# Sums over eight selections as trees of three contiguous additions

## The chip, the cores and the metric

One core of a Trainium2 chip. The metric is the device time of one execution in microseconds (us), the median of three runs.

## The reference

One encoder layer on 1024 tokens of width 1024, in float32: a combined projection, two groups of attention heads (windowed, and on a 2-D neighbourhood), an output projection and a layer norm; then PEER, a layer of 16384 single-neuron experts with product keys, and a second layer norm. PEER is where the edit lies. For each token and each of 8 heads two sets of 128 scores are cut to their top 16; the 256 sums of pairs are cut to their top 16 again, and each of these 16 names one expert:

```
cand_idx = i_top[:, :, 0, :, None] * PEER_N_KEYS + i_top[:, :, 1, None, :]
fs, fpos = lax.top_k(cand, PEER_TOPK)
eidx = jnp.take_along_axis(cand_idx, fpos, axis=-1)
g = jax.nn.softmax(fs, axis=-1)
```

The output of PEER is the sum over a token's 128 experts of gelu(x . u) * g * v.

## The kernel before

The tokens are eight tiles of 128, one token a partition. The first part of the kernel projects, attends (two tiles at a time) and normalizes. After each pair of tiles `route` (L519) computes the scores of PEER for the pair, takes the top 16 of each set with `top16` (L122) and calls `decode` (L176) for each of the two tiles. Route of pair 0 comes before the attention of tiles 2 and 3, and so on; route of pair 3 is the last of this part.

The experts are computed in two ways. Tiles 0 to 4 (`ND` = 5) go through all experts densely: a matrix of gates, nearly all of it zero, is multiplied in between two matmuls (`hstage` L707, `vmm` L733). For tiles 0 and 1 (`NS` = 2) this matrix is written in DRAM (`gs`) by `scatter` (L160): 256 indirect DMAs issued by GpSimd, each adding 128 single gates at the computed places, 16 for each tile and head, the heads of both tiles in turn (L576 to L578). For tiles 2 to 4 `build` (L582) makes it with one-hot matmuls and stores it in `gd` (L617). Tiles 5 to 7 gather their experts' rows one by one with indirect DMAs (L656) during the dense part, and VectorE multiplies and adds them.

The dense part starts with `load_g` (L696): on SyncE's queue a load of gates from `gs`, which waits for the scatters of every head, and one from `gd`. The raw blocks of the experts' weights (L709, L727) follow on the same queue. ScalarE casts a block (L86), VectorE subtracts (L87), and TensorE multiplies (L91 to L93, L736 to L738).

In `decode` everything but one exponential is VectorE's. It makes a table of the candidates (L183, L185), takes their top 16 and positions (L190), and turns a position into the index of an expert by selections. Sixteen steps compare all positions with the starts of the rows and multiply with a difference of indices (L203; the first is L201), sixteen others pick the index of the second key (L217). Each writes one of the eight slices of `big` (128 partitions x 8 slices x 8 heads x 16); after every eight a reduction sums over the slices (L206, L221) into `ef` or `e2`. The slices lie 512 bytes apart, and the reduction reads them with the slice as the innermost dimension:

```
bsum = big.rearrange("p a h k -> p h k a")
...
if a % 8 == 7:
    nc.vector.tensor_reduce(ef if a == 7 else e2, bsum, AX.X, OP.add)
```

`big`, `ef` and `e2` have one buffer each, which every call of `decode` uses. A call has four reductions, and there are eight calls. L207 and L222 add the two halves; L210 to L215 split the sum in row and remainder; L224 (tiles 2 to 7) or L226 and L227 (tiles 0 and 1) write the indices.

The order of the instructions on each engine isn't that of the text: it is laid out when the program is built, by a planner with durations of its own for every instruction (L859, `schedule_with_timeline_sim=True`). VectorE's instructions of `decode` stand in it between those of attention, `top16`, `build` and the start of the dense part. On the chip each engine then keeps to its order.

Of the kernel before, what the change touches and what calls it, by code (L numbers as in the profile page):

```python
# [17 lines left out]
OP = mybir.AluOpType  # L18
AX = mybir.AxisListType
# [38 lines left out]
def trunk(ctx, tc, x, xt, wqk, wo, gn, sink, biasa, biasb, ln, wq, keyst, uv, ut, vt, out):  # L58
    nc = tc.nc
# [62 lines left out]
    def top16(vals, idx, src, pool, n):  # L122
        tmp = pool.tile([P, P], F32, name="t16")
        nc.vector.max(vals[:, 0:8], src)
        nc.vector.max_index(idx[:, 0:8], vals[:, 0:8], src)
        nc.vector.match_replace(tmp[:, :n], vals[:, 0:8], src, BIG)
        nc.vector.max(vals[:, 8:16], tmp[:, :n])
        nc.vector.max_index(idx[:, 8:16], vals[:, 8:16], tmp[:, :n])
# [47 lines left out]
    def decode(idx, g, sv, iv, pool, t=None):  # L176
        s2 = sv.rearrange("p (h two) k -> p h two k", two=2)
        fi = pool.tile([P, 8, 2, TOPK], F32, name="fi", bufs=1)
        nc.vector.tensor_copy(fi, iv.rearrange("p (h two) k -> p h two k", two=2))
        cv = pool.tile([P, 8, NCAND], F32, name="cv", bufs=1)  # L180
        for a in range(8):
            w = WIDTHS[a]
            nc.vector.tensor_tensor(cv[:, :, OFFS[a]:OFFS[a] + w], s2[:, :, 1, 0:w],  # L183
                                    s2[:, :, 0, a:a + 1].to_broadcast([P, 8, w]), OP.add)
        nc.vector.tensor_tensor(cv[:, :, NCAND - 8:], s2[:, :, 0, 8:16],  # L185
                                s2[:, :, 1, 0:1].to_broadcast([P, 8, 8]), OP.add)
        fs = pool.tile([P, 8, TOPK], F32, name="fs", bufs=1)
        pos = pool.tile([P, 8, TOPK], U32, name="pos", bufs=1)
        for h in range(8):
            top16(fs[:, h, :], pos[:, h, :], cv[:, h, :], pool, NCAND)  # L190
        pf = pool.tile([P, 8, TOPK], F32, name="pf", bufs=1)
        nc.vector.tensor_copy(pf, pos)
        dlt = pool.tile([P, 8, TOPK - 1], F32, name="dlt", bufs=1)
        nc.vector.tensor_sub(dlt, fi[:, :, 0, 1:], fi[:, :, 0, 0:TOPK - 1])
        nc.vector.scalar_tensor_tensor(dlt, dlt, 64.0, wrow[:, None, :].to_broadcast([P, 8, TOPK - 1]),
                                       op0=OP.mult, op1=OP.add)
        big = pool.tile([P, 8, 8, TOPK], F32, name="big", bufs=1)
        ef = pool.tile([P, 8, TOPK], F32, name="ef", bufs=1)
        e2 = pool.tile([P, 8, TOPK], F32, name="e2", bufs=1)
        bsum = big.rearrange("p a h k -> p h k a")  # L200
        nc.vector.tensor_scalar(big[:, 0, :, :], fi[:, :, 0, 0:1].to_broadcast([P, 8, TOPK]), 64.0, None, op0=OP.mult)  # L201
        for a in range(1, TOPK):
            nc.vector.scalar_tensor_tensor(big[:, a % 8, :, :], pf, START[a] - 0.5,  # L203
                                           dlt[:, :, a - 1:a].to_broadcast([P, 8, TOPK]), op0=OP.is_ge, op1=OP.mult)
            if a % 8 == 7:
                nc.vector.tensor_reduce(ef if a == 7 else e2, bsum, AX.X, OP.add)  # L206
        nc.vector.tensor_add(ef, ef, e2)  # L207
        ei = pool.tile([P, 2, 8 * TOPK], I32, name="ei", bufs=1)
        e0 = ef.rearrange("p h k -> p (h k)")
        nc.vector.tensor_copy(ei[:, 0, :], e0)  # L210
        nc.vector.tensor_scalar(ei[:, 1, :], ei[:, 0, :], 63, None, op0=OP.bitwise_and)
        nc.vector.tensor_scalar(ei[:, 0, :], ei[:, 0, :], 6, 7, op0=OP.logical_shift_right, op1=OP.logical_shift_left)
        of = pool.tile([P, 2, 8, TOPK], F32, name="of", bufs=1)
        nc.vector.tensor_copy(of.rearrange("p a h k -> p a (h k)"), ei)
        nc.vector.tensor_sub(pf, pf, of[:, 1])  # L215
        for b in range(TOPK):
            nc.vector.scalar_tensor_tensor(big[:, b % 8, :, :], pf, float(b),  # L217
                                           fi[:, :, 1, b:b + 1].to_broadcast([P, 8, TOPK]),
                                           op0=OP.is_equal, op1=OP.mult)
            if b % 8 == 7:  # L220
                nc.vector.tensor_reduce(ef if b == 7 else e2, bsum, AX.X, OP.add)  # L221
        nc.vector.tensor_add(ef, ef, e2)  # L222
        if t is None:
            nc.vector.tensor_add(idx.rearrange("p (h k) -> p h k", h=8), ef, of[:, 0])  # L224
        else:
            nc.vector.tensor_scalar(ef, ef, float(P * GC), base[:, t:t + 1], op0=OP.mult, op1=OP.add)  # L226
            nc.vector.scalar_tensor_tensor(idx.rearrange("p (h k) -> p h k", h=8), of[:, 0], GC / P, ef,  # L227
                                           op0=OP.mult, op1=OP.add)
        gv = g.rearrange("p (h k) -> p h k", h=8)
        nc.vector.tensor_tensor(gv, fs, fs[:, :, 0:1].to_broadcast([P, 8, TOPK]), OP.subtract)  # L230
        nc.scalar.activation(g, g, AF.Exp)
        gs = pool.tile([P, 8], F32, name="gs")
        nc.vector.tensor_reduce(gs, gv, AX.X, OP.add)
        nc.vector.reciprocal(gs, gs)
        nc.vector.tensor_mul(gv, gv, gs[:, :, None].to_broadcast([P, 8, TOPK]))
# [4 lines left out]
    with ExitStack() as att:  # L240
# [278 lines left out]
        def route(pr):  # L519
# [48 lines left out]
            for t in tiles:  # L568
                if t >= ND:
                    decode(eidx[t], gate[t], stop_[t], itop[t], rs)  # L570
                    continue
                idx = rs.tile([P, P], I32, name="idxd", bufs=4)
                g = rs.tile([P, P], F32, name="gated", bufs=4)
                decode(idx, g, stop_[t], itop[t], rs, t if t < NS else None)
                (dense if t < NS else todo).append((t, idx, g))
# [99 lines left out]
    total = NG * P // NB  # L675
# [31 lines left out]
    def hstage(e, pend):  # L707
        raw = dn.tile([P, KT, P], F32, name="raw", bufs=3)
        nc.sync.dma_start(raw, ut[e])  # L709
        uh = dn.tile([P, KT, P], F32R, name="uh")  # L710
        ul = dn.tile([P, KT, P], F32R, name="ul")
        split(uh, ul, raw)
        gl = dn.tile([P, DN], F32, name="gl")
        for j, (o, n) in enumerate(hch):
            ps = ph.tile([P, 512], F32, name="h")
            for k in range(KT):
                mm3(ps[:, :n], uh[:, k, :], ul[:, k, :], dh[:, k, o:o + n], dl[:, k, o:o + n], k == 0, k == KT - 1)
            nc.scalar.activation(gl[:, o:o + n], ps[:, :n], AF.Gelu)  # L718
            if j == (e == ne - 1) and pend is not None:
                vres(*pend)  # L720
        glv = gl.rearrange("p (q c) -> p q c", c=GC)
        nc.vector.tensor_mul(glv, glv, gt[e // EG][:, :, e % EG, :])
        ah = dn.tile([P, DN], F32R, name="ah", bufs=3)
        al = dn.tile([P, DN], F32R, name="al", bufs=3)
        split(ah, al, gl)
        raw = dn.tile([P, D], F32, name="raw", bufs=3)
        nc.sync.dma_start(raw, vt[e * P:(e + 1) * P, :])  # L727
        vh = dn.tile([P, D], F32R, name="vh", bufs=3)
        vl = dn.tile([P, D], F32R, name="vl", bufs=3)
        split(vh, vl, raw)  # L730
        return ah, al, vh, vl
# [39 lines left out]
    for e in range(ne):  # L771
        if e % EG == 0 and e + EG < ne:
            load_g(e // EG + 1)
        a = hstage(e, pend)
# [88 lines left out]
```

## Time and profile before

| | |
|---|---|
| median of three runs | 2978.63 us (2978.54 to 2978.84) |
| the profiled execution | 2985.32 us |
| its span, first to last instruction | 2981.6 us |
| mean granted clock of TensorE | 0.961 |
| TensorE busy | 2733.9 us (92%) |
| VectorE busy | 2408.1 us (81%) |
| ScalarE busy | 1202.3 us (40%) |
| GpSimd busy | 1065.1 us (36%) |

The profile is of one execution; its span is the time from the first to the last instruction of the program, and 3.7 us of its time lie outside it. Busy shares are means over the whole span, in which the parts of the kernel differ much, so the rows below are mostly of single stretches. In the rows PE is TensorE, DVE VectorE, ACT ScalarE, POOL GpSimd, SP SyncE; a q behind the name is the engine's sequencer, which issues DMAs and waits.

### The profile page before, as it was taken

How to read it: one execution, taken by the hardware profiler on the slowest of the kernel's cores; microseconds unless marked ns; L12 is line 12 of the kernel's file. 1: busy time of each engine (PE TensorE's matmuls, PEld its weight loads, DVE VectorE, ACT ScalarE, POOL GpSimd, SP SyncE). 2: the span in 40 equal slices, each digit the busy share in tenths (PEclk: the TensorE clock that was granted, in tenths of full speed). 3: DMA queues.
4: the chain of work that ended last, by engine and by line, in shares of the span. 5: the costliest groups of instructions: out<-in, count | busy, mean ns of one | idle time of the engine just before them, and what ended most of it. 6: DMA issues, size and time to landing. Idle time of an engine off the chain costs nothing.

```text
span 2981.6 us, 43327 instructions
## 1 busy us (share of the span) xinstructions
PE 2733.9 (92%) x15569; PEld 2357.3 (79%) x15569; DVE 2408.1 (81%) x5427; ACT 1202.3 (40%) x2486; POOL 1065.1 (36%) x732
## 2 busy tenths in 40 slices
PE   6887899897997867999999999999999999999996
PEld 4776577575785766888998899898888898988885
DVE  2344267887979988898998989999989999998965
ACT  2343154342786762333333343333333333333332
POOL 1111001078888881333333323333333333333300
PEclk8998989898997988999999999999999999999998
DMA  7688598897977767988998989998998898998851
GB/s 233 200 271 269 177 322 296 260 262 180 267 223 221 220 161 265 348 331 324 353 331 332 332 329 335 336 347 334 330 344 327 321 353 322 342 349 332 329 210 46
DMA packets 384886, 854.37 MB, mean 287 GB/s; under 512 B 83616, under 2 KB 243360, under 8 KB 333728
## 3 DMA queue, kind: packets, MB, share of 16 engines
q0 software_dynamic: 124224, 433.43, 41.3%
q1 hardware_dynamic: 230816, 388.82, 38.5%
q10 hardware_dynamic: 29632, 29.37, 3.1%
q8 instruction: 122, 2.00, 0.3%
q14 instruction: 92, 0.75, 0.1%
HBM read 765.21 MB, written 86.11 MB: 286 GB/s over the span
## 4 chain that ended last, share of the span: by engine, by line
PE 48%; DVE 5%; DMA 4%; issue 3%; ACT 2%; POOL 1%; SPq 0%; ACTq 0%; POOLq 0%; DVEq 0%
PE h L91 9%; PE h L92 8%; PE h L93 8%; PE po L736 5%; PE po L737 5%; PE po L738 5%; PE fl L737 3%; PE fl L736 3%; PE fl L738 3%; DMA uv<-in_uv_dram,eidx 2%; DMA raw<-in_ut_dram 2%; DVE uv L658 1%; DVE acc L668 1%; POOL uv L656 1%; DVE vl L87 1%
## 5 line engine op out<-in xcount | busy, mean ns | idle before, releaser
L656 POOL DMA_INDIRECT uv<-in_uv_dram,eidx x384 | 570.4, 1486 | 1162.5 <-DVE acc L668 688.5
L91 PE MATMUL h<-dh,uh 128*128 128x320 f32 x2048 | 641.3, 313 | 49.0 <-ACT uh L86 25.6
L93 PE MATMUL h<-dh,ul 128*128 128x320 f32 x2048 | 634.6, 310 | 0.8 <-DVE ul L87 0.8
L92 PE MATMUL h<-dl,uh 128*128 128x320 f32 x2048 | 634.1, 310 | 0.0
L658 DVE SCALAR_TENSOR_TENSOR uv<-uv,xg 128x1024 f32<-128x1024 f32 x384 | 467.4, 1218 | 43.1 <-DMA uv<-in_uv_dram,eidx 37.3
L165 POOL DMA_INDIRECT gs<-gated,idxd x256 | 434.9, 1699 | 171.3 <-DMA qlo<-wqd 87.0
L668 DVE SCALAR_TENSOR_TENSOR acc<-uv,hh,acc 128x1024 f32<-128x1024 f32 x381 | 487.6, 1280 | 4.3
L91 PEld LDWEIGHTS h<-dh,uh 128*128 128x128 f32 x2048 | 385.7, 188 | 83.7 <-ACT gl L718 48.6
L92 PEld LDWEIGHTS h<-dl,uh 128*128 128x128 f32 x2048 | 385.9, 188 | 10.9
L93 PEld LDWEIGHTS h<-dh,ul 128*128 128x128 f32 x2048 | 385.7, 188 | 4.9 <-DVE ul L87 1.5
L736 PE MATMUL po<-vh,ah 128*128 128x512 f32 x768 | 288.2, 391 | 1.5 <-ACT ah L86 1.5
L737 PE MATMUL po<-vl,ah 128*128 128x512 f32 x768 | 287.8, 391 | 0.0
L662 ACT ACTIVATE hh<-hh 128x1 f32<-128x1 f32 x384 | 77.6, 202 | 476.3 <-DVE uv L658 474.9
L738 PE MATMUL po<-vh,al 128*128 128x512 f32 x768 | 260.8, 391 | 0.0
L764 ACT COPY fl<-fl 128x512 f32<-128x512 f32 x252 | 147.1, 584 | 278.7 <-PE fl L738 278.5
L765 DVE TENSOR_TENSOR facc<-facc,fl 128x512 f32<-128x512 f32 x252 | 172.6, 685 | 72.8 <-ACT fl L764 72.6
L718 ACT ACTIVATE gl<-h 128x320 f32<-128x320 f32 x256 | 111.4, 435 | 254.5 <-PE h L93 244.4
L736 PE MATMUL fl<-vh,ah 128*128 128x512 f32 x512 | 201.8, 394 | 3.0 <-ACT fl L764 3.0
L737 PE MATMUL fl<-vl,ah 128*128 128x512 f32 x512 | 201.9, 394 | 0.0
L738 PE MATMUL fl<-vh,al 128*128 128x512 f32 x512 | 199.6, 390 | 0.0
L87 DVE TENSOR_TENSOR ul<-raw,uh 128x1024 fp32r<-128x1024 f32 x128 | 156.1, 1220 | 52.6 <-ACT uh L86 51.7
L86 ACT CAST uh<-raw 128x1024 fp32r<-128x1024 f32 x128 | 134.2, 1049 | 116.8 <-DMA raw<-in_ut_dram 60.7
(201 smaller groups left out, 5389.2 us busy)
## 6 DMA issues: line engine op xcount, KB each, us to landing
raw<-in_ut_dram SPq DMA_DIRECT2D x128, 512.0 KB
raw<-in_vt_dram SPq DMA_DIRECT2D x128, 512.0 KB
qhi<-wqd SPq DMA_DIRECT2D x48, 512.0 KB
qlo<-wqd SPq DMA_DIRECT2D x48, 512.0 KB
gd<-stage SPq DMA_DIRECT2D x12, 2048.0 KB
gt<-gd SPq DMA_DIRECT2D x32, 768.0 KB
wraw<-in_wqk_dram SPq DMA_DIRECT2D x36, 512.0 KB
bt<-in_biasb_dram SPq DMA_DIRECT2D x64, 288.0 KB
```

The lines of the kernel that those rows point to most:

```text
L87: nc.vector.tensor_sub(lo, raw, f(hi))
L91: nc.tensor.matmul(ps, wh, mh, start=first, stop=False)
L92: nc.tensor.matmul(ps, wh, ml, start=False, stop=False)
L93: nc.tensor.matmul(ps, wl, mh, start=False, stop=last)
L165: st = nc.gpsimd.indirect_dma_start(out=gs, out_offset=bass.IndirectOffsetOnAxis(ap=idx[:, k:k + 1], axis=0), in_=g[:, k:k + 1], in_offset ...
L656: nc.gpsimd.indirect_dma_start(out=u, out_offset=None, in_=uv, in_offset=bass.IndirectOffsetOnAxis(ap=eidx[t][:, k:k + 1], axis=0))
L658: nc.vector.scalar_tensor_tensor(u[:, 0:D], u[:, 0:D], 1.0, x1[t], op0=OP.mult, op1=OP.mult, accum_out=hh[:, k:k + 1])
L668: nc.vector.scalar_tensor_tensor(acc, u[:, D:], hh[:, k:k + 1], acc, op0=OP.mult, op1=OP.add)
L736: nc.tensor.matmul(ps, ah[:, cs], vh[:, js], start=first, stop=False)
L737: nc.tensor.matmul(ps, ah[:, cs], vl[:, js], start=False, stop=False)
L738: nc.tensor.matmul(ps, al[:, cs], vh[:, js], start=False, stop=last)
L765: nc.vector.tensor_add(acc[:, j, :], acc[:, j, :], fl)
```

## The change

Each of the two reductions at L206 and L221 becomes a call of a local function `total`, which adds the upper four slices of `big` onto the lower four, then the upper two of these onto the lower two, and then the two that are left into the destination. All three are additions on VectorE, over 512, 256 and 128 contiguous elements of each partition, and each reads what the one before it wrote. The view `bsum` goes. The sums are those of before, in another order.

```
-        bsum = big.rearrange("p a h k -> p h k a")
+
+        def total(dst):
+            nc.vector.tensor_add(big[:, 0:4], big[:, 0:4], big[:, 4:8])
+            nc.vector.tensor_add(big[:, 0:2], big[:, 0:2], big[:, 2:4])
+            nc.vector.tensor_add(dst, big[:, 0], big[:, 1])
+
...
             if a % 8 == 7:
-                nc.vector.tensor_reduce(ef if a == 7 else e2, bsum, AX.X, OP.add)
+                total(ef if a == 7 else e2)
...
             if b % 8 == 7:
-                nc.vector.tensor_reduce(ef if b == 7 else e2, bsum, AX.X, OP.add)
+                total(ef if b == 7 else e2)
```

## Rows read from the trace of the kernel before

**Rows 1.** Windows: us, then each engine's busy time (instructions), clock, DMA share, GB/s.

```profile
556.40:597.40 41.00, 35.82 (x254) 29.35 (x253) 41.00 (x199) 16.84 (x38) 0.00 (x0) 0.88 0.96 303
597.40:1107.70 510.30, 426.71 (x2893) 355.65 (x2891) 440.56 (x1861) 324.31 (x765) 427.11 (x252) 0.92 0.79 219
...
1133.30:1160.00 26.70, 22.84 (x119) 20.82 (x120) 24.94 (x52) 9.25 (x12) 0.90 (x1) 0.88 0.39 129
1200.00:2900.00 1700.00, 1680.02 (x9349) 1513.81 (x9348) 1540.91 (x2242) 612.34 (x1224) 554.17 (x372) 1.00 0.90 331
```

**Rows 2.** Chain that ended last, 1112 to 1132 us: start, us, what.

```profile
1112.73 1.55 POOL gs L165
...
1114.59 4.18 DMA gs<-gated,idxd
...
1119.07 0.37 SPq L700
...
1124.24 7.67 DMA raw<-in_ut_dram
```

**Rows 3.** Timeline of PE, after 1107 us: start, us, ..., [idle before <-releaser].

```profile
1133.34 0.64 PE L91 MATMUL h<-dh,uh 128*128 128x320 f32 x1 [25.65 <-ACT uh L86]
...
1159.62 0.41 PE L91 MATMUL h<-dh,uh 128*128 128x320 f32 x1 [1.57 <-ACT gl L718]
```

**Rows 4.** Timelines of DVE and POOL, 596 to 608 us.

```profile
596.37 0.28 DVE L227 SCALAR_TENSOR_TENSOR idxd<-of,ef 128x128 int32<-128x128 f32 x1
...
603.24 1.69 DVE L203 SCALAR_TENSOR_TENSOR big<-pf,dlt 128x128 f32<-128x128 f32 x8
...
605.38 1.91 DVE L206 TENSOR_REDUCE e<-big 128x128 f32<-128x1024 f32 x1
...
597.48 2.10 POOL L165 DMA_INDIRECT gs<-gated,idxd  x1 [87.00 <-DMA qlo<-wqd]
...
603.61 2.75 POOL L165 DMA_INDIRECT gs<-gated,idxd  x1 [0.31 <-issue]
606.66 1.55 POOL L165 DMA_INDIRECT gs<-gated,idxd  x1 [0.30 <-issue]
```

**Rows 5.** Line L165: xcount, duration ns min/median/max, first and last start.

```profile
L165 POOL DMA_INDIRECT gs<-gated,idxd x256: 1543/1547/5346, 597.5 to 1114.6; - x128
```

**Rows 6.** Groups from 597.4 to 1116.8 us: busy us, mean ns, idle before.

```profile
L165 POOL DMA_INDIRECT gs<-gated,idxd x256 | 434.9, 1699 | 171.3 <-DMA qlo<-wqd 87.0 <-issue 81.3 <-DMA gs<-gated,idxd 2.7
...
L203 DVE SCALAR_TENSOR_TENSOR big<-pf,dlt 128x128 f32<-128x128 f32 x87 | 18.4, 276 | 0.0
...
L206 DVE TENSOR_REDUCE e<-big 128x128 f32<-128x1024 f32 x6 | 11.4, 1897 | 0.0
```

**Rows 7.** Groups of DVE over the whole span.

```profile
L606 DVE TENSOR_TENSOR qj<-iota,tt 128x512 f32<-128x512 f32 x96 | 65.4, 681 | 0.0
...
L206 DVE TENSOR_REDUCE ef<-big 128x128 f32<-128x1024 f32 x8 | 15.2, 1904 | 0.0
...
L207 DVE TENSOR_TENSOR ef<-ef,e 128x128 f32<-128x128 f32 x8 | 2.2, 271 | 0.0
```

**Rows 8.** Timelines of DVE and ACT, 1151 to 1160 us (tile 7).

```profile
1151.84 1.98 DVE L221 TENSOR_REDUCE ef<-big 128x128 f32<-128x1024 f32 x1
1153.86 1.70 DVE L217 SCALAR_TENSOR_TENSOR big<-pf,fi 128x128 f32<-128x128 f32 x8
...
1157.95 0.29 DVE L224 TENSOR_TENSOR eidx<-ef,of 128x128 int32<-128x128 f32 x1
...
1159.13 0.44 ACT L718 ACTIVATE gl<-h 128x320 f32<-128x320 f32 x1 [8.90 <-DVE eidx L224]
```

**Rows 9.** Timeline of DVE, 572 to 575 us (tile 0).

```profile
572.29 0.21 DVE L210 CAST ei<-ef 128x128 int32<-128x128 f32 x1
...
573.77 0.20 DVE L211 TENSOR_SCALAR ei<-ei 128x128 int32<-128x128 int32 x1
...
574.26 0.20 DVE L212 TENSOR_SCALAR ei<-ei 128x128 int32<-128x128 int32 x1
```

## The prediction

> **What bounds the kernel now.** I read the trace by stages first. The decode of the expert choices, where the edit lies, runs between 556 and 1158 us of the span; from 1200 us on TensorE is busy for 1680.0 of 1700 us, so a gain or a loss here moves the end by as much as that last stage starts earlier or later, and nothing else counts [rows 1]. In 556 to 597 us VectorE has no idle time; from 597 to 1108 it is busy for 440.6 of 510.3 us and TensorE for 426.7, neither full, and GpSimd for 427.1 [rows 1]. None looks full, so the busy shares do not say which of them holds up the next stage.
>
> The chain of waits tells it: the last indirect scatter-add on GpSimd, its landing, the loads of the gates on SyncE, which wait for every scatter, and behind them on the same queue the first raw block, 7.67 us on its way [rows 2]. TensorE stands still for 25.65 us until that block has been cast [rows 3]. So VectorE, which is through with its work for TensorE by then, is not the bound; the scatters are. They form one almost unbroken line of 256, from 597.48 to the landing at 1118.77 us, and the first starts 0.8 us after VectorE has written the indices of tile 0 (L227 at 596.37) [rows 2, 4]. The time of the end is thus: end of tile 0's decode, plus the line of scatters, plus a fixed restart.
>
> What does a scatter cost? The median is 1.547 us [rows 5], with some 0.3 us before the next [rows 4], but the mean is 1.699 [rows 6]: 434.9 - 256 x 1.547 = 38.9 us are lost over the line. Put beside VectorE's timeline the loss shows its cause. The scatter at 603.61 us starts within a run of eight L203, each of which reads two operands in SBUF (pf and dlt); the run ends at 604.93 and the scatter takes 2.75, which is 1.2 us more than 1.55 and about what was left of the run. The scatter at 606.66 lies over a strided reduction, which reads one operand, and takes 1.55 [rows 4]. A scatter that starts while VectorE works with two operands from SBUF waits for it; over a reduction it does not.
>
> **The change part by part.** Each of 32 reductions (four a tile, eight tiles), 1.90 us [rows 7], becomes three additions over 512, 256 and 128 elements a partition. 512 cost 0.68 (L606) and 128 cost 0.27 (L207) [rows 7]; 256 are not shown, and between these two lies 0.41. Together 1.36 us. Operations that need not wait overlap: eight L203 of 0.276 take 1.69 us, so each start comes 0.07 before the end of the last [rows 4, 6]; directly dependent ones start 0.04 after it (L221 at 1151.84 ends at 1153.82, L217 starts at 1153.86) [rows 8]. So a tree takes 1.15 us of VectorE with other work between its steps and 1.44 without, against 1.83 to 1.94: a saving of 0.50 to 0.68 each, 16 to 22 us of VectorE's time. Nothing changes on the queues of SyncE, ScalarE and GpSimd: the edit issues no transfer. The waits it adds are those of each addition on the one before; behind them in order on VectorE stand attention and top-16 work of later tiles.
>
> (a) Four trees of tile 0 lie ahead of the first scatter, in the stretch where VectorE is full. Kept in place they bring it 4 x 0.68 = 2.7 us forward. But each tree has two more steps that wait for a step before. The order on VectorE is laid out ahead of time, and it puts work of other tiles between dependent steps: between L211 and L212 of tile 0 lie 0.49 - 0.13 = 0.36 us of it, between L210 and L211 1.48 - 0.14 = 1.34 [rows 9]. Eight new places at some 0.3 us, the shorter of these, give back 2.4. I take -0.3 us; the ends are -2.7 (no such work) and 8 x 0.85 - 2.7 = +4.1 us (the mean of the two).
>
> (b) 22 reductions lie in the stretch of the scatters: the group of six here and three more like it, of six, five and five [rows 6]. They held nothing up; 22 trees with two operands from SBUF will. Scatters start every 517.1 / 255 = 2.03 us (the first at 597.48, the last at 1114.59 [rows 2, 4]). One that starts at random within a hold of r us waits r/2 on average, and r / 2.03 of the starts fall in it, so a hold costs r x r / 4.06. Three holds of their own: (0.46 + 0.17 + 0.07) / 4.06 = 0.17 us a tree, 3.8 in all; one hold of 1.36: 0.46 a tree, 10.0 in all. Dependent additions leave a gap, so it should lie nearer the lower end: I take +5.0. The lower end is 0, if the starts happen to miss them.
>
> The Trainium skill bears on this. Its page SBUF — State Buffer, section Who interferes with whom, says that a VectorE instruction with two SBUF inputs contends with a GpSimd instruction that reads SBUF and that tensor_reduce on this chip never does; but it also infers that tensor_tensor leaves descriptor generation alone. By the first (b) is a loss, by the second nothing, and the sum would be -1.8 in place of +3.2 us; the two scatters above agree with the first.
>
> (c) The four trees of tile 7 lie after the restart. Its last index (L224 at 1157.95) releases a load on ScalarE, which held up the activation at 1159.13 for 8.90 us [rows 8], and TensorE waited 1.57 us for that [rows 3]. The four save some 2.0 us, of which TensorE can win back the 1.57: -1.5. The lower end is all of TensorE's idle time there, 26.7 - 22.84 = 3.9 us [rows 1], the upper +2.0, if work put into the new places undoes the saving and as much again.
>
> The 24 other trees free some 14 us of VectorE between 597 and 1130 us: worth nothing, since the scatters cover it; without that cover they would count. Nor do I count that the next batch could write four of the eight slices after the first addition.
>
> Sum: -0.3 + 5.0 - 1.5 = +3.2 us. Against the profiled execution, 2985.32 us (its span is 2981.6), that is 2988.5; the median of the runs shown is 2978.63, 6.7 below it, so I say 2981.8. About 0.2% (6.0 us) is what can be told from no change.
>
> **Rivals.** First, the scatters are not lengthened, and tile 0 comes early in full: -2.7 + 0 - 1.5 = -4.2, 2974.4 us, and up to 6.6 us faster with all idle time of (c). For it speaks that some runs of VectorE miss the starts; against it the 38.9 us lost already. The inference on the Trainium skill's page SBUF — State Buffer, section Who interferes with whom, comes to this rival. Second, on the slower side, the holds join: an addition beside a run of L203 or L602 and L606 makes one long hold, and the line of scatters grows by 10.0 or more. -0.3 + 10.0 - 1.5 = +8.2, 2986.8 us. It decides the case from (b) = 7.8 on, or 0.35 us a tree. For it speaks that a run of eight L203 was kept together and cost one scatter 1.2 us; against it the gap between dependent steps. Third, the layout puts more into the eight places of tile 0: +4.1 + 5.0 - 1.5 = +7.6, 2986.2 us. For it speaks that no two dependent steps of that decode shown stand side by side. Fourth, the change does not shorten VectorE's work: 1.44 against 1.90 would have to be wrong by a third; then (a) is the +2.4 of the new places, (c) is nothing, and with (b) it is +7.4, 2986.0 us.
>
> **How the numbers follow.** The forecast 0.48, the first rival 0.24, the second 0.13, the third 0.11, the fourth 0.04. Of the first some 0.17 lies beyond 6.0 us, an order laid out anew that also wins elsewhere among it; with the second, third and fourth in full and 0.03 from the upper part of the forecast, slower has 0.31; 0.52 is left for no change. The range goes from -6.6 (2972) to +13.4 (2992), short of all three upper ends at once.
>
> **What would show it.** Right: L206 and L221 gone, three groups of 32 at 0.68, 0.41 and 0.27 us; the first scatter between 595 and 598 us; the mean scatter up from 1.699 to about 1.72, its median still 1.547; the scatters longer than that lying over additions; TensorE's restart near 1138. Wrong: a mean scatter at 1.70 or below, a first scatter after 600 us, or a restart that no longer follows the landing of the last scatter.

## The result, and the profile after

The changed kernel takes 2998.47 us (median of 4 runs, 2991.39 to 3005.57); the kernel before, run beside it on the same chip, 2978.59. The ratio is 1.0075, with a 95% interval of 1.0055 to 1.0095: slower by some 20 us, beyond the upper end of the range. The profiled execution took 2991.39 us, its span is 2989.6.

First the stages; the columns are those of [rows 1]. The second window runs from the first to the last start of a scatter, while that of [rows 1] ends earlier, when TensorE runs out of work.

```profile
556.40:597.40 41.00, 38.69 (x283) 32.51 (x284) 39.54 (x207) 18.97 (x44) 0.00 (x0) 0.92 0.94 300
597.40:1126.20 528.80, 417.94 (x2851) 343.76 (x2849) 448.82 (x2015) 322.37 (x758) 444.36 (x255) 0.89 0.77 212
...
1200.00:2900.00 1700.00, 1682.48 (x9367) 1516.01 (x9366) 1540.50 (x2243) 613.64 (x1226) 559.46 (x372) 1.00 0.90 331
```

The last stage is as full as it was. From the first to the last start of a scatter lie 528.7 us in place of 517.1 [rows 5]. The chain of waits of the changed kernel has the same links as [rows 2], each later:

```profile
1124.37 1.55 POOL gs L165
1126.22 2.97 DMA gs<-gated,idxd
1130.54 2.12 SPq L705
1132.70 1.71 SPq L710
1134.45 7.71 DMA raw<-in_ut_dram
```

TensorE's timeline shows the end of that chain (compare [rows 3]):

```profile
1143.66 0.63 PE L91 MATMUL h<-dh,uh 128*128 128x320 f32 x1 [53.56 <-ACT uh L86]
```

TensorE stood still for 53.56 us where it had been 25.65, and restarted 10.3 us later. It had run out of other work 17.6 us earlier than before (at 1090.1 in place of 1107.7), which helped nothing. The line of scatters (columns as in [rows 5]):

```profile
L165 POOL DMA_INDIRECT gs<-gated,idxd x256: 1542/1547/7719, 597.5 to 1126.2; - x128
```

The median is still 1.547 us and the first start still 597.5, but the last start comes 11.6 us later, and the longest scatter takes 7.72 us. The groups of VectorE, to be held against [rows 7]:

```profile
L611 DVE TENSOR_TENSOR qj<-iota,tt 128x512 f32<-128x512 f32 x96 | 65.8, 685 | 0.0
...
L202 DVE TENSOR_TENSOR big<-big 128x512 f32<-128x512 f32 x32 | 21.9, 684 | 0.1
...
L203 DVE TENSOR_TENSOR big<-big 128x256 f32<-128x256 f32 x32 | 13.3, 416 | 0.1
...
L204 DVE TENSOR_TENSOR ef<-big 128x128 f32<-128x128 f32 x16 | 4.6, 285 | 0.0
```

So the change does what it says: three additions of 684, 416 and some 283 ns in place of 1.90 us. VectorE's busy time over the span fell from 2408.1 to 2387.9 us. It became 20 us less busy, and the kernel 20 us slower.

Now the scatter of 7.72 us. These are lines of the timelines of GpSimd and of VectorE around it; VectorE's begin in the fourth line.

```profile
947.27 4.81 POOL L165 DMA_INDIRECT gs<-gated,idxd  x1 [0.31 <-issue]
952.38 7.72 POOL L165 DMA_INDIRECT gs<-gated,idxd  x1 [0.30 <-issue]
960.41 1.55 POOL L165 DMA_INDIRECT gs<-gated,idxd  x1 [0.30 <-issue]
...
952.38 0.68 DVE L202 TENSOR_TENSOR big<-big 128x512 f32<-128x512 f32 x1
952.98 0.29 DVE L179 CAST fi<-itop 128x256 f32<-128x256 uint32 x1
...
953.32 0.42 DVE L203 TENSOR_TENSOR big<-big 128x256 f32<-128x256 f32 x1
...
954.44 0.22 DVE L206 TENSOR_SCALAR big<-fi 128x128 f32<-128x128 f32 x1
...
957.40 0.69 DVE L607 TENSOR_TENSOR pi<-iota,tt 128x512 f32<-128x512 f32 x1
958.00 0.68 DVE L611 TENSOR_TENSOR qj<-iota,tt 128x512 f32<-128x512 f32 x1
958.60 0.48 DVE L124 MAX8 stop<-sc 128x8 f32<-128x128 f32 x2
```

The scatter starts with the first addition of a tree. From there to L124 VectorE has no idle gap; additions, a subtraction, selections, comparisons, two casts and a multiplication by a constant (L206) follow one another. The casts and L206 read one operand, and yet the scatter was not let go at them. L124, which reads one operand, starts at 958.60, and the scatter ends 1.50 us after that: it has waited for the whole stretch. In the kernel before a strided reduction stood in the place of each tree, and the scatter that lay over one was not held [rows 4].

### The profile page after: what moved, and what is told of

Same layout as the page of the kernel before. It is cut to its first block, busy times and chain, and to the rows that moved or that the text cites. A ratio compares the mean times of both kernels' runs of the same rounds, so it can differ in the third digit from the quotient of the medians.

```text
span 2989.6 us, 43399 instructions
## 1 busy us (share of the span) xinstructions
PE 2731.6 (91%) x15569; PEld 2350.4 (79%) x15569; DVE 2387.9 (80%) x5491; ACT 1202.1 (40%) x2486; POOL 1080.4 (36%) x732
## 4 chain that ended last, share of the span: by engine, by line
PE 54%; DVE 3%; DMA 2%; ACT 2%; issue 1%; POOL 0%; SPq 0%; ACTq 0%; POOLq 0%; DVEq 0%
PE h L91 10%; PE h L92 9%; PE h L93 9%; PE po L741 5%; PE po L742 5%; PE po L743 5%; PE fl L741 4%; PE fl L742 4%; PE fl L743 3%; DMA raw<-in_ut_dram 1%; DMA uv<-in_uv_dram,eidx 1%; DVE uv L663 1%; ACT uh L86 0%; ACT gl L723 0%; ACT vh L86 0%
## 5 line engine op out<-in xcount | busy, mean ns | idle before, releaser
L165 POOL DMA_INDIRECT gs<-gated,idxd x256 | 445.9, 1742 | 177.9 <-DVE big L203 93.5
```

What stands on the lines that cost most here:

```text
L165: st = nc.gpsimd.indirect_dma_start(out=gs, out_offset=bass.IndirectOffsetOnAxis(ap=idx[:, k:k + 1], axis=0), in_=g[:, k:k + 1], in_offset ...
```

## The experiments

The theories, by the letters that the expectations use. **A**: the additions read two operands in SBUF and hold up the scatters. **B**: the loss comes from the new order in which all work is laid out on VectorE, not from the additions' operands. **C**: it arises at TensorE's restart or in tile 7. **D**: it is only spread between executions.

In the table, decode is the time from the first decode instruction of tile 0 (the cast into `fi`) to its index write; line is from the first to the last start of the 256 scatters; idx 6 is when the index of tile 6 is written; dense is from TensorE's restart to its last instruction. All are from the one profiled execution of each kernel, in us.

| kernel | decode | first scatter | line | mean scatter | idx 6 | dense |
|---|---|---|---|---|---|---|
| before | 62.4 | 597.5 | 517.1 | 1.699 | 1129.5 | 1828.6 |
| before, again (c1) | 62.4 | 583.4 | 514.9 | 1.688 | 1118.8 | 1827.3 |
| changed | 68.9 | 597.5 | 528.7 | 1.742 | 1101.0 | 1826.2 |
| changed, again (e4) | 71.1 | 598.1 | 523.2 | 1.715 | 1105.3 | 1823.8 |
| contiguous reduction (e1) | 61.7 | 587.8 | 509.3 | 1.671 | 1119.1 | 1826.3 |
| trees in tiles 0, 7 (e2) | 69.3 | 603.4 | 516.3 | 1.702 | 1158.3 | 1844.3 |
| trees in tiles 1 to 6 (e3) | 62.4 | 588.2 | 526.6 | 1.736 | 1104.6 | 1836.7 |
| trees in tile 0 (f1) | 70.4 | 595.4 | 521.9 | 1.716 | 1156.0 | 1851.0 |
| trees in tile 7 (f2) | 62.4 | 597.1 | 513.2 | 1.681 | 1132.6 | 1828.9 |
| one-operand extras (d1) | 62.9 | 589.4 | 535.1 | 1.737 | 1150.6 | 1839.8 |
| two-operand extras (d2) | 62.4 | 589.2 | 533.9 | 1.728 | 1159.6 | 1840.2 |

**The four runs first made.** e1 keeps the reduction and lays `big` out so that it is contiguous:

```
-        big = pool.tile([P, 8, 8, TOPK], F32, name="big", bufs=1)
+        big = pool.tile([P, 8, TOPK, 8], F32, name="big", bufs=1)
...
-            nc.vector.scalar_tensor_tensor(big[:, a % 8, :, :], pf, START[a] - 0.5,
+            nc.vector.scalar_tensor_tensor(big[:, :, :, a % 8], pf, START[a] - 0.5,
...
-                nc.vector.tensor_reduce(ef if a == 7 else e2, bsum, AX.X, OP.add)
+                nc.vector.tensor_reduce(ef if a == 7 else e2, big, AX.X, OP.add)
```

> The slices lie innermost in big, so that one contiguous reduction of 1024 elements (one operand) takes the place of the strided one; no trees. Theory A (two-operand additions hold up the scatters): the reduction takes 1.1 to 1.3 us, saves as much of VectorE as the trees, and holds up nothing: mean scatter 1.68 to 1.72, last scatter starts at 1108 to 1117, time 2970 to 2981. Theory B (a new order of the instructions, from any shorter sum, does the harm): mean scatter 1.73 or more, time 2990 or more.

e2 and e3 use the trees in some tiles and the strided reduction in the others, e4 is the changed kernel once more:

```
+            if not tree:
+                nc.vector.tensor_reduce(dst, big.rearrange("p a h k -> p h k a"), AX.X, OP.add)
+                return
```

> Trees in the decode of tiles 0 and 7 alone, which lie outside the line of scatters; strided reductions in tiles 1 to 6. Theory A: mean scatter 1.68 to 1.72, time 2973 to 2980. Theory C (the harm is at the restart, in tile 7's decode): as slow as the changed kernel, 2990 to 3005, with a mean scatter as before.

> Trees in tiles 1 to 6 alone, strided reductions in tiles 0 and 7. Theory A: mean scatter 1.73 to 1.78, last scatter starts 8 to 25 us later than before, time 2988 to 3006. Theory C: mean scatter may rise, but the time stays within 2975 to 2983.

> The changed kernel once more. Theory A: times again spread in steps of several us between 2988 and 3006, and the profile's mean scatter and last scatter differ from those of its first profile by as much as its time does. Theory D (the spread comes from something else than the scatters): the line of scatters has the same length as in the first profile, within 1 us, whatever the time.

Measured, as ratios to the kernel before: e1 0.9992 (0.9978 to 1.0006), e2 1.0076 (1.0054 to 1.0097), e3 1.0071 (1.0045 to 1.0096), e4 1.006 (1.0032 to 1.0088). The loss repeats, which D does not allow. It does not add up over tiles: the trees of tiles 1 to 6 cost as much as all, and so do those of 0 and 7. In e3 the line is long and tile 0's decode is as before; in e2 the line is as before, and tile 0's decode is 7 us longer. In both the dense part is longer too, by 9 and 16 us, which it is not in the whole change; A expected 2973 to 2980 us of e2, and its 3002.84 is what C expected. More than one cause, then, and A names only one.

In e1 the mean scatter is the shortest but one of all runs of the encoder, and its line is 6.7 us shorter than the mean of the two traces of the kernel before; the time gained nothing that can be told from noise. Its groups of VectorE show one price of the new layout:

```profile
L216 DVE SCALAR_TENSOR_TENSOR big<-pf,fi 128x128 f32<-128x128 f32 x128 | 33.3, 411 | 0.1
...
L220 DVE TENSOR_REDUCE e<-big 128x128 f32<-128x1024 f32 x8 | 9.8, 1225 | 0.0
```

The reduction fell from 1.90 to 1.2 us, but each selection, which now writes with a stride, rose from 0.276 [rows 6] to 0.41. The chain of waits shows another reason. In e1 the restart did not wait for the last scatter, which started at 1097.0, but for the last store of the gates that `build` makes for tiles 2 to 4 (`gd`); behind its landing comes the first load of gates on SyncE's queue:

```profile
1100.94 6.26 DMA gd<-stage
1107.40 0.37 SPq L699
```

In the trace of the kernel before that store was issued at 1109.12. With the same 6.26 us to its landing (an estimate) it was through at 1115.4, 3.4 us before the last scatter landed at 1118.77 [rows 2]. So a second path lay close behind the scatters.

**Without the scatters.** n1 is the kernel before and n2 the changed one, both without the scatters into the gates of tiles 0 and 1:

```
-            for h in range(8):
-                for t, idx, g in dense:
-                    scatter(t, h, idx, g)
```

> The kernel before without its scatters: the gates of tiles 0 and 1 are left out (their dense experts get zero gates), all else stays. Theory A (the scatters set the restart, and holds by two-operand work stretch their line): the restart comes earlier, 1105 to 1128 us, time 2955 to 2975, and the executions agree within 2 us. Theory C (the dense part after the restart is what differs and spreads): the spread of several us stays.

> The changed kernel without its scatters, as the run above. Theory A: VectorE's saving is now open: as fast as the kernel before without scatters or up to 18 us faster, and the executions agree within 2 us. Theory C: 8 to 25 us slower than the kernel before without scatters, with a spread.

n1 took 2971.36 us, n2 2964.86: 0.9997 (0.9975 to 1.0019) and 0.9965 (0.9944 to 0.9986) of the kernel before. Where nothing waits for a scatter, the change is 6.5 us faster. Its loss lies on the path of the scatters: in when they start, or in how long they take. But n1 itself is not faster than the kernel before. Its TensorE restarts 596.7 us after tile 0's decode began, against 599.4 and 600.0 with the scatters: the store of `gd` landed at 1102.96 there, and the first load of gates followed at 1103.17. The scatters led that second path by some 3 us only. Tile 0's decode was 73.5 us long in n2 and 62.4 in n1, and there nobody waited for it. The executions of n1 and n2 still spread by 14 and 17 us, so the spread does not need the scatters.

**Early raw blocks.** p1 is e1 and p2 the changed kernel, with the first three raw blocks of the dense stage asked for ahead of the gates' loads on SyncE:

```
+    for which, e in (("u", 0), ("v", 0), ("u", 1)):
+        early[which, e] = fetch(which, e)
     load_g(0)
```

> The contiguous reduction, and in addition the first three raw blocks of weights (two of ut, one of vt) are loaded ahead of the first loads of the gates on SyncE's queue, so that the restart doesn't wait for the scatters. Theory A: TensorE's long idle time shrinks from 24 to under 17 us and the time falls to 2955 to 2970. If the first gates hold up TensorE after one block anyway, 2968 to 2975.

> The changed kernel with the same three early blocks. Theory A: part of the longer line is covered by the work on the first blocks, 2975 to 2992, but it stays slower than the contiguous reduction with early blocks by 8 us or more. Theory C: the loss of 17 to 20 us stays in full.

p1 took 2969.59 us, 0.9973 (0.9952 to 0.9995): it beats both kernels. p2 is at 1.0028 (1.0007 to 1.0049); some of the loss is covered, the line of scatters is not shortened (its last start is at 1126.9). p0 below gives the kernel before the same.

**Extras with one and two operands.** To part A from B, three instructions without use were laid behind each of the 24 reductions of tiles 1 to 6, of about the same durations in both kernels:

```
+        def more():
+            nc.vector.bn_stats(bst[:, 0, :], flat[:, 0:512])
...
+        def more():
+            nc.vector.tensor_add(big[:, 0:4], big[:, 0:4], big[:, 4:8])
...
                 nc.vector.tensor_reduce(ef if a == 7 else e2, bsum, AX.X, OP.add)
+                if extra:
+                    more()
```

> The kernel before with three more VectorE instructions, without use for the result, behind each of the 24 reductions of tiles 1 to 6: statistics (one operand) over 512, 256 and 128 elements, into a tile of their own. The reductions stay. Theory A (two SBUF operands hold up the scatters): about 33 us more of VectorE's work, none of which holds a scatter; mean scatter as before, 1.69 to 1.71 us, none longer than 4 us; restart of TensorE within 3 us of 1133; time within 0.3% of the kernel before unless VectorE itself becomes the bound. Rival B (it is the amount of work put on VectorE, or the new order of its instructions): mean scatter and restart move as in the changed kernel, 1.72 to 1.74 us and 1139 to 1144.

> The same with the three additions of the change as the extra instructions (two SBUF operands, over 512, 256 and 128 elements, in place in the tile that the reduction has read), the reductions kept. Theory A: mean scatter 1.73 to 1.76 us, one or more scatters above 4 us, last scatter and restart 8 to 14 us later than in the run with the one-operand extras, time 0.3 to 0.6% above that run. Rival B: no difference between the two runs by more than 3 us at the restart, and mean scatters equal within 0.02 us.

> The kernel before, with the first three raw blocks of the dense stage asked for on SyncE ahead of the loads of the gates, as in the two runs with early raw blocks. If what stood between the last scatter and TensorE is the gates' loads and the raw block behind them, TensorE's 25.65 us of idle time split and shrink to some 13 to 16, and the time falls 0.2 to 0.4% against the kernel before; then the contiguous reduction has next to nothing in the run that beat both kernels. If the gain there came from both, this run is within 0.15% of the kernel before.

> The kernel before, once more, for a second trace: how far do the line of scatters and the restart move from one execution to the next without any change? Theory A wants its mean scatter below 1.71 us, and its restart between 1129 and 1137 us; a mean of 1.72 or more would put the difference of the changed kernel within the scatter of executions.

d1 is at 1.0079 (1.0052 to 1.0106), d2 at 1.0086 (1.0061 to 1.011). **A fails here as it stood**: the one-operand extras lengthen the line as much, 535.1 us. What was expected for B came true on each count: d1's mean scatter is 1.737 us and its restart at 1143.1, and the two runs differ by 2.4 us at the restart and by 0.009 us in the mean scatter. No addition lies over d1's scatters; what holds them are selections and comparisons of the old kind, which the new order has put elsewhere, and GpSimd sits idle three times for 3.5 to 6.1 us before a scatter, twice without a releaser in the profile and once for the landing of scatters before it (the idle times between the scatters sum to 92.4 us, 84.3 in the kernel before). In both, the index of tile 6, like that of tile 7, is written only after TensorE's restart, and the dense part is 11 to 12 us longer. So an order laid out anew can cost as much as the additions do; how much of each is in the change, these two runs do not show. p0 came to 0.9985 (0.9967 to 1.0003), between the two cases expected; whether e1's reduction has a part in p1's gain is not settled.

c1 teaches how such traces are to be compared. In the same kernel the first scatter starts at 583.4 in place of 597.5. The decode itself took the same; it began earlier. The cast into `fi` and the index write of tile 0, on VectorE's timeline, first in c1, then in the changed kernel:

```profile
519.91 0.27 DVE L179 CAST fi<-itop 128x256 f32<-128x256 uint32 x1
...
582.31 0.28 DVE L227 SCALAR_TENSOR_TENSOR idxd<-of,ef 128x128 int32<-128x128 f32 x1
```

```profile
527.50 0.28 DVE L179 CAST fi<-itop 128x256 f32<-128x256 uint32 x1
...
596.42 0.27 DVE L232 SCALAR_TENSOR_TENSOR idxd<-of,ef 128x128 int32<-128x128 f32 x1
```

62.4 against 68.9 us. In the kernel before as profiled the decode had begun at 533.99, 6.5 us later than in the changed one, and that hid the 6.5 us exactly: the first scatter stood at 597.5 in both.

**One tile alone.** f1 has the trees in tile 0 only, f2 in tile 7 only (`tree=t == 0` and `tree=t == 7` in the calls).

> Trees in tile 0 alone, reductions in the other seven. Theory A' (the trees of tile 0 open eight more places between steps that wait for one another, into which the order on VectorE puts work of other tiles): from tile 0's first decode instruction to its index write 68 to 73 us in place of 62.4, the first scatter 6 to 11 us later by that; the line of 256 scatters 514 to 518 us and its mean 1.69 to 1.71, as in the kernel before; time 0.2 to 0.4% above it. Rival (the loss lies in the line of scatters alone): 62 to 63 us, and the time within 0.1%.

> Trees in tile 7 alone. Tile 0's decode 62.4 us and the line of scatters 514 to 518 us as in the kernel before; from TensorE's restart to its end 1 to 4 us shorter than the 1828 of the kernel before if the prediction's step on tile 7 was right, 10 or more longer if the trees of tile 7 are what lengthened that stretch in the run with trees in tiles 0 and 7. Time within 0.15% of the kernel before in the first case.

f1 is at 1.01 (1.0072 to 1.0129), no faster than the whole change: four trees are enough. The decode took 70.4 us as expected. The line was not as expected, 521.9 us with no addition in it. And the dense part is 23 us longer, which is most of f1's loss and is no part of that of the whole change. Some 8 us of this are two waits of TensorE after the restart, and the rest is not placed; under them, tile 6's index on VectorE:

```profile
1146.54 0.63 PE L91 MATMUL h<-dh,uh 128*128 128x320 f32 x1 [5.41 <-ACT gl L726]
1154.56 0.42 PE L91 MATMUL h<-dh,uh 128*128 128x320 f32 x1 [2.74 <-ACT gl L726]
```

```profile
1156.01 0.28 DVE L232 TENSOR_TENSOR eidx<-ef,of 128x128 int32<-128x128 f32 x1
```

Tile 6's index, written before the restart in the kernel before, now falls into the dense stage. The four kernels with a late idx 6 (f1, e2, d1, d2) are those with the longest dense parts; that one makes the other was not tried. In the full change tile 6 is early. f2 is at 0.9999 (0.9983 to 1.0015), with everything as in the kernel before: tile 7 takes no part in the loss.

**The hold by itself.** m1 and m2 leave the encoder out. They are 128 scatters, in groups of 16, beside fixed patterns of VectorE work, in a fixed order. Patterns of m2 (the last two put other work between the steps of a tree):

```
+    def tree(fill):
+        chain(nc.vector.tensor_add(big[:, 0:4], big[:, 0:4], big[:, 4:8]))
+        fill()
+        chain(nc.vector.tensor_add(big[:, 0:2], big[:, 0:2], big[:, 2:4]))
+        fill()
+        chain(nc.vector.tensor_add(ef, big[:, 0], big[:, 1]))
```

> Only 128 indirect scatter-adds, in eight groups of 16, each group beside one fixed pattern of VectorE work, started together; the whole encoder is left out. Groups 1 and 7: VectorE idle. 2: strided reductions end to end. 3: statistics over 512 end to end (one operand). 4 and 8: the tree of the change, each followed by one reduction. 5: eight selections (two SBUF operands), each eight followed by a reduction. 6: eight selections and a tree in turn, with no one-operand instruction between. Theory A: scatters take 1.55 us in groups 1, 2, 3 and 7; in 4 and 8 some take up to 3.0 (a tree of 1.44 us holds whoever starts under it until its end, the 0.04 us between dependent additions not enough to slip in); in 5 up to 3.3; in 6 a scatter is held far longer than one tree, to the end of the unbroken stretch or nearly. Rival (the gaps between dependent additions let the scatter go): group 4 at most 2.3 us, group 6 at most 3.3. Rival B (two operands have nothing to do with it): all groups equal.

> Again only 128 scatters in eight groups of 16 beside patterns of VectorE work; the encoder is left out. The run before of this kind held no scatter longer than 2.05 us, and its dependent instructions left 34 ns of idle VectorE between them. Groups: 1 VectorE idle; 2 eight selections on whole operands, then a reduction (as group 5 there); 3 the same with the second operand spread over the row as in the kernel (one value per head, read 16 times); 4 six of the kernel's comparisons over 512 elements (both operands spread) end to end, then a reduction; 5 six contiguous additions over 512 that do not depend on each other, then a reduction; 6 the bare tree, then a reduction; 7 the tree with four spread selections between each two of its steps, then a reduction; 8 the tree with two spread comparisons between its steps, then a reduction. Theory G (a scatter is let go by an idle gap on VectorE or by an instruction that leaves it alone; work laid between the steps of a tree closes the gaps): at most 2.1 us in groups 1, 2 and 6, up to 4 us or more in 4 and 5, and 3 to 4.5 us in 7 and 8. Rival S (it is the spread operands that hold, contiguous additions do not): long scatters in 3, 4, 7 and 8, none above 2.1 in 5 and 6. Rival N (neither: the long holds of the kernel come from something that these patterns lack): none above 2.1 in any group.

m1 was a miss for A: no scatter took over 2.05 us, the tree with selections in turn (group 6) 1.83 at most. Its timeline of both engines, in the group of bare trees:

```profile
179.56 0.69 DVE L205 TENSOR_TENSOR big<-big 128x512 f32<-128x512 f32 x1
179.63 2.04 POOL L165 DMA_INDIRECT gs<-g,idx  x1 [0.30 <-issue]
180.28 0.43 DVE L206 TENSOR_TENSOR big<-big 128x256 f32<-128x256 f32 x1
```

The scatter is held for 0.5 us, about to the end of the first addition, behind which VectorE idles for 0.03 us. Reductions and statistics held none (1.54 to 1.55 us). In m2, group 5 (six independent additions) and group 7 (a tree with selections between its steps):

```profile
233.53 3.68 DVE L225 TENSOR_TENSOR pi<-big 128x512 f32<-128x512 f32 x6
233.59 5.04 POOL L165 DMA_INDIRECT gs<-g,idx  x1 [0.30 <-issue]
237.14 1.85 DVE L209 TENSOR_REDUCE e<-sel 128x128 f32<-128x1024 f32 x1
238.93 3.68 DVE L225 TENSOR_TENSOR pi<-big 128x512 f32<-128x512 f32 x6
238.94 5.09 POOL L165 DMA_INDIRECT gs<-g,idx  x1 [0.30 <-issue]
...
312.40 0.68 DVE L228 TENSOR_TENSOR big<-big 128x512 f32<-128x512 f32 x1
312.43 4.23 POOL L165 DMA_INDIRECT gs<-g,idx  x1 [0.30 <-issue]
...
315.16 1.87 DVE L209 TENSOR_REDUCE e<-sel 128x128 f32<-128x1024 f32 x1
```

The longest scatters are as G expected them, but for group 8, which goes above its 4.5: the bare tree 1.80 us at most, the filled trees 4.23 and 5.03, contiguous additions and spread comparisons alike 5.09. The held scatter is let go when the reduction starts, and ends during it; the next then starts just as the next run of additions does, and is held again.

Yet G is too strong as a rule. Earlier in group 5, scatters that start further into a run of additions pass while it goes on, without an idle gap and without a reduction:

```profile
222.71 3.72 DVE L225 TENSOR_TENSOR pi<-big 128x512 f32<-128x512 f32 x6
223.38 2.02 POOL L165 DMA_INDIRECT gs<-g,idx  x1 [0.31 <-issue]
225.71 1.54 POOL L165 DMA_INDIRECT gs<-g,idx  x1 [0.30 <-issue]
```

The first starts 0.67 us into the run and ends 1 us before it does. So whether it is the 0.03 us of idle time that lets the scatters of m1 go is not shown either. In groups 4 and 5 those held for the whole run are the ones that start within 0.06 us of its beginning. And runs of eight selections, which have two operands too, held no scatter for long: 1.90 us at most in m1 and in groups 2 and 3 of m2. What decides who passes is not settled.

## Why the prediction was wrong, point by point

**What bounds the kernel** was read rightly for both kernels: the end followed tile 0's decode, the line of scatters and the restart, and without the scatters the change wins 6.5 us (n2 against n1). Two things were missed. The store of `gd` lay some 3 us behind the scatters (n1, e1), so scatters that came earlier could have won little. And the restart was not fixed: from the last start of a scatter it took 18.8 and 21.7 us in the two traces of the kernel before, 17.4 and 17.6 in those of the changed one.

**(a) is the step that failed.** The prediction put eight new places in tile 0's decode "at some 0.3 us" and took -0.3 us, with an upper end of +4.1. The steps of the trees of tile 0 in the second trace of the changed kernel (e4), VectorE's timeline:

```profile
560.03 0.67 DVE L202 TENSOR_TENSOR big<-big 128x512 f32<-128x512 f32 x1
...
561.96 0.41 DVE L203 TENSOR_TENSOR big<-big 128x256 f32<-128x256 f32 x1
...
564.07 0.27 DVE L204 TENSOR_TENSOR e<-big 128x128 f32<-128x128 f32 x1
```

Between the first end (560.70) and the second start lie 1.26 us, between the second end (562.37) and the third start 1.70. The eight places of the four trees sum to 12.0 us in the changed kernel and to 14.3 in e4, 1.5 to 1.8 each, five to six times what was taken and some twice the mean of the two places read from [rows 9]. Not all of it is work: for 1.5 and 3.8 us of the decode VectorE stands idle, where it never did in the two traces of the kernel before. The decode is 6.5 and 8.7 us longer; without the idle time that is 5 us in both, the work that came in less what the trees save. What came in is largely top-16 work on other tiles' scores, some of attention, and seven selections of another decode. The groups of VectorE from the cast to the index write, in c1:

```profile
L125 DVE FIND_INDEX8 itop<-stop,sc 128x8 uint32<-128x128 f32 x6 | 1.6, 275 | 0.0
...
L126 DVE MATCH_REPLACE8 t<-stop,sc 128x128 f32<-128x128 f32 x4 | 1.1, 266 | 0.0
...
L127 DVE MAX8 stop<-t 128x8 f32<-128x128 f32 x2 | 0.4, 248 | 0.0
```

and in e4:

```profile
L457 DVE CUSTOM_DVE_ANT_0 s<-ps,bt 128x288 f32<-128x288 f32 x8 | 3.5, 440 | 3.8 <-PE ps L386 3.8
...
L125 DVE FIND_INDEX8 itop<-stop,sc 128x8 uint32<-128x128 f32 x8 | 2.2, 282 | 0.0
...
L126 DVE MATCH_REPLACE8 t<-stop,sc 128x128 f32<-128x128 f32 x8 | 2.2, 273 | 0.0
...
L127 DVE MAX8 stop<-t 128x8 f32<-128x128 f32 x8 | 2.0, 279 | 0.0
```

So in e4 the work laid into the stretch was not even ready: VectorE's 3.8 us are a wait for TensorE. This is the third rival, whose price of +4.1 was too low against the +7.6 measured (means of two traces). All six traces of kernels with trees in tile 0 show it (68.0 to 73.5 us), none of the ten others does (61.7 to 63.0); f1 shows it with those four trees alone.

**(b) had the right mechanism in part and half the size.** +5.0 was forecast; the line took 528.7 and 523.2 us in the two traces of the changed kernel against 517.1 and 514.9, so +10.0 between the means. The mean scatter is 1.742 and 1.715 in place of "about 1.72". The argument that "dependent additions leave a gap, so it should lie nearer the lower end" is right of a bare tree (m1) and wrong of a tree in this kernel, where other work stands between its steps and the holds can join (m2, and the scatter of 7.72 us). That is the second rival, given 0.13. GpSimd's idle time between the scatters is as before (84.3 and 85.8 us, against 84.3 and 84.2), so nearly all of the 10 us lies in the scatters' own durations. In each trace of the changed kernel some 33 scatters start within unbroken two-operand work that holds a tree's addition, and these lose 22 and 17 us. Not all of this is added, since the other scatters lose less (28 and 26 us, against 38.9 in the kernel before), probably because the joined stretches have taken in comparisons that held scatters already. And the new order alone lengthens the line as well, by some 6 us in f1 and by 19 in d1, where nothing with additions lies over it (one trace each; the two traces of the kernel before differ by 2.2 us, those of the changed one by 5.5). How much of the 10 us is the additions' and how much the order's is not settled. The prediction's rule, too, that a scatter which starts under two operands from SBUF waits for the work, was too broad: it was read from one such scatter, and though the kernel's traces have more of the kind, in m2 spread selections like the kernel's cost 0.14 us at most.

The Trainium skill's page SBUF — State Buffer, section Who interferes with whom, infers that tensor_tensor leaves descriptor generation alone; the first rival's nothing for (b) agrees with that. Here scatters under additions and comparisons took up to 5.09 us in place of 1.55, so for these indirect transfers the measurement decides against the inference, and for the rule on two SBUF inputs of the same page of the Trainium skill. That section of the Trainium skill says of VectorE's 2-port modes that whoever issues first has the shared pair for the whole instruction; in m2 scatters were held over six additions in a row.

**(c)**: -1.5 was forecast. In f2, TensorE's wait of 1.57 us [rows 3] is gone (0.53 is left in its place), and the dense part is 1828.9 us all the same, as before, so no gain is seen there. With the whole change it was 1826.2 and 1823.8 us, 3.0 below the means of the kernel before.

**The sum.** By means of two traces each: decode +7.6, line +10.0, dense -3.0, start of the decode -0.3, last scatter to restart -2.7, together +11.6; the spans differ by 2986.0 - 2974.3 = 11.7. By that alone the time would lie within the range, whose upper end is +13.4. The timed runs differ by 19.9 and, in e4, by 16.0. The 4 to 8 us between stay open: the profiled executions of the changed kernel are the fastest of four and the second fastest of six, 7.1 and 8.2 us below the median of theirs, and no trace shows what the slower ones lose.

**What was to be seen.** The first scatter at 597.5 lay within "595 to 598" by luck, since the decode had begun 6.5 us earlier. TensorE's restart came at 1143.7 and 1138.9, the second only as forecast. The saving on VectorE was right (16 to 22 us forecast, 20.2 measured), and so was that it is worth nothing between 597 and 1130 us.

## What to carry to other kernels

Before a long instruction is split into dependent short ones, look at who fills the places between them: on an engine whose order is laid out ahead, each new place costs what the planner finds to put there and what that has to wait for (1.5 to 1.8 us here), and on the path that sets the end this outweighs the instructions' own saving. A one-operand reduction can be worth its time as a break that lets GpSimd through; a tree of additions takes that break away. Measure a stage from its own first instruction, not from the start of the span.

## What was not expected of the hardware

An indirect scatter-add that starts under VectorE work with two SBUF operands can be held for many instructions in place of one: 1.55 us alone, 2.05 at most under a bare tree, 4.23 to 5.09 under joined work, 7.72 in the kernel. It was let go at the end of an addition with 0.03 us of idle time behind it (m1), at a reduction (m2) and at MAX8 (the kernel); two casts and a multiplication by a constant, with one operand each, did not let it go. But not every scatter under such work is held: in groups 4 and 5 of m2 some pass with more additions or comparisons to come (1.54 to 2.03 us), and selections alone cost 0.35 us at most. Where a scatter passed over selections in 1.54 us, it was the selection that took longer (0.33 to 0.34 us in place of 0.28, groups 2 and 3 of m2). Held scatters fall into step with the pattern that holds them, so that four to six in a row are late (m2), and a mean over random starts can misjudge the sum. And the same kernel reached its first scatter at 583.4 us in one execution and 597.5 in another.
